# First head's block doubling planned later, the combination of the dilated groups spread out, a third work tile for the merge logits

## Chip, core and metric

One Trainium2 chip, one of its cores. The metric is the device time of one execution of the whole layer in microseconds (us), as the median of several runs. The input is x of 1 x 1024 x 1024 float32, the output has the same shape.

## What is computed

```python
x = x + 1/2 * SwiGLU_1(RMSNorm(x))
h = RMSNorm(x); cols = h @ w_in
A = dilated causal window attention   # 3 groups: window 128, 512, 2048 at dilation 1, 4, 16; 4 heads of 64 each
    # the three groups are weighted by their log-denominators:
    # y = sum_g softmax_g(lse_g) * o_g, per head
B = gated DeltaNet, 8 heads of 128, chunks of 64
    # per chunk: M = strict_lower(kbeta k^T * decay); u, w = (I + M)^-1 [vbeta, kbeta exp(g)]
    # scan: v_new = u - w S;  o = q_dec S + a_qk v_new;  S = exp(g_last) S + k_dec^T v_new
y = (sigmoid(g_a) * (A @ w_branch_a) + sigmoid(g_b) * (B @ w_branch_b)) @ w_out
x = x + y;  x = x + 1/2 * SwiGLU_2(RMSNorm(x));  final RMSNorm
```

All products are float32. The kernel splits an operand into a rounded high part and a low rest (H, L in the names) and adds three products HH, LH, HL, each a TensorE matmul of 128 x 128 on 512 columns.

## The kernel before, in words

The stages follow one another: FFN 1 (to about 735 us of the span), the mixer (to about 1790), `merge_out` (to about 2000), FFN 2.

**The mixer** has one loop of bulk work and a set of small tasks. Bulk work is `proj` (L229): a projection of h by 128 columns of w_in, 24 matmuls for each half of the tokens. Tasks are Python generators: attention blocks, `combine`, and for each DeltaNet head keys, decay, solve, scan and output. A planner (`Weave`) holds a planned time that each TensorE instruction advances by a cost written beside it. After every 9 or 12 bulk matmuls it runs the tasks that are due; a task issues its instructions up to its next `yield`, and the yielded number is how many planned us later it is due again. TensorE (PE) runs in exactly the order that comes out. The other engines' rows are ordered by priority (attention and `combine` first, then head 0, head 1, ..., bulk last). Each engine, and the DMA queue of SyncE (SP), executes its rows in order, so a row that waits holds up all rows behind it.

**One head** (h) goes: keys are projected, convolved (L927, DVE) and squared; `gdn_decay` makes Dm (cumulative sums on PE L1001, Exp on ACT L1003); `products` makes N (PE L1017, DVE L1019). `gdn_inverse_blocks` inverts the 32 x 32 diagonal blocks of all chunks: it stores N's blocks (L1075), loads them transposed into a tile M (SP, L1078), runs 68 small DVE rows, each on the result of the one before (L1087, L1088, L1100, L1101), stores the inverse (SP, L1109), loads it back as U (SP, L1114), and transposes U on DVE into Tm (L1116). M and Tm are made from the same tag "Tm", which has one buffer: M of head h + 1 can be loaded only when head h has read its Tm for the last time. `gdn_solve` then yields 57, scales two tiles (L1053), yields 5, and `gdn_merge` doubles the blocks to 64 and 128: PE L1136, DVE L1138, PE L1143, DVE L1145 and L1146, PE L1153 (the last reader of Tm), DVE L1155, PE L1161. Then w (PE L1061, ACT L1062) and the scan of 8 chunks (PE L1228, L1232, L1238, L1245; DVE L1230, L1243, L1249). PE's small products go to a few PSUM banks by tag: "tA" (L934, L1001, L1017, L1061, L838), "tM" for the doubling, "tC" for the scan; a bank is free again when DVE or ACT has read it. Results of L1017 are read by L1019.

**combine** weights the three groups of the attention, 8 tiles of 128 tokens. A tile loads oc (L815, two buffers of tag "xs"), runs 14 DVE rows (L820 to L834) and one Exp, yields 12, transposes on PE (L838), copies on ACT (L841) and stores (L842). It starts only once head 1 has its U, and pauses while a head is being made ready (`C.segs`, decay or values outstanding).

**merge_out** runs two halves of the tokens (a = 0, 1). For each of 8 columns f it loads the gate logits of both branches into a tile sgl (L1430, L1431; two buffers, tag "xs") and branch A's product (L1433), takes the sigmoid (ACT L1434), multiplies by B @ w_branch_b on PE, and adds on DVE (L1437 to L1439); the sum is split into mH (ACT L236) and mL (DVE L237), the last reader of sgl. Then 4 x 2 groups of 24 matmuls by w_out (PE L1456) read mH and mL, whose eighth column block f = 7 they need last. Weights come through `load_w2` (L203 load, L204 high part on ACT, L205 low part on DVE).

Of the kernel before, what the change touches and what calls it, by code (L numbers as in the profile page):

```python
# [9 lines left out]
F32 = mybir.dt.float32  # L10
# [6 lines left out]
P = 128  # L17
# [72 lines left out]
def psum(C, tag):  # L90
    return C.pp.tile([P, 512], F32, name=tag, tag=tag, bufs=BANKS[tag])
# [711 lines left out]
def combine(C):  # L803

    nc = C.nc
    while not C.attended or len(C.heads) < 2 or C.heads[1].U is None:
        yield 1.0
    for t in range(NT):

        while C.segs or any(X.D is None and X.ready for X in C.heads) or sum(not X.vals[1] for X in C.heads) > 1:  # L810
            yield 1.0
        C.combining = True
        oc = C.tp.tile([P, 792], F32, name="oc", tag="xs", bufs=2).rearrange("p (g q f) -> p g q f", g=3, q=2)
        for g in range(3):
            nc.sync.dma_start(oc[:, g], C.od[g][t * P:t * P + P])  # L815
        m, l = oc[:, :, :, 128:130], oc[:, :, :, 130:132]
        M = C.mx.tile([P, 1, 2, 2], F32, name="cM", tag="cM", bufs=2)
        e = C.mx.tile([P, 3, 2, 2], F32, name="ce", tag="ce", bufs=2)
        z = C.mx.tile([P, 3, 2, 2], F32, name="cz", tag="cz", bufs=2)
        nc.vector.tensor_tensor(out=M, in0=m[:, 0:1], in1=m[:, 1:2], op=ALU.max)  # L820
        nc.vector.tensor_tensor(out=M, in0=M, in1=m[:, 2:3], op=ALU.max)
        nc.vector.tensor_tensor(out=e, in0=m, in1=M.to_broadcast([P, 3, 2, 2]), op=ALU.subtract)
        nc.scalar.activation(e, e, AF.Exp, scale=0.125)
        nc.vector.tensor_tensor(out=z, in0=e, in1=l, op=ALU.mult)
        nc.vector.tensor_tensor(out=M, in0=z[:, 0:1], in1=z[:, 1:2], op=ALU.add)
        nc.vector.tensor_tensor(out=M, in0=M, in1=z[:, 2:3], op=ALU.add)
        nc.vector.reciprocal(M, M)
        nc.vector.tensor_tensor(out=e, in0=e, in1=M.to_broadcast([P, 3, 2, 2]), op=ALU.mult)
        for q in range(2):
            ov = oc[:, :, q, 0:128].rearrange("p g (h d) -> p g h d", d=64)  # L830
            nc.vector.tensor_tensor(out=ov, in0=ov, in1=e[:, :, q, :].unsqueeze(3).to_broadcast([P, 3, 2, 64]), op=ALU.mult)
        y = oc[:, 0, :, 0:128]
        for g in (1, 2):
            nc.vector.tensor_tensor(out=y, in0=y, in1=oc[:, g, :, 0:128], op=ALU.add)  # L834
        yield 12.0
        ps = psum(C, "tA")
        for f in range(2):
            C.weave.pe(nc.tensor.transpose(ps[:, f * P:f * P + P], y[:, f, :], C.ident), 0.11)  # L838
        C.combining = False
        yT = C.mx.tile([P, 2, P], F32, name="yT", tag="sc", bufs=6)  # L840
        nc.scalar.copy(yT, ps[:, :256].rearrange("p (f t) -> p f t", t=P))  # L841
        nc.sync.dma_start(C.yad[:, :, t * P:t * P + P], yT)  # L842


def gate_tile(C, w_in, c0, dst):
# [163 lines left out]
def products(C, X, src, sign):  # L1009

    nc = C.nc
    dst = t4c(C, "ka")
    for q in range(2):
        ps = psum(C, "tA")
        for i in range(4):
            c = q * 4 + i
            C.weave.pe(nc.tensor.matmul(ps[:, i * P:i * P + P], X.k[:, c, :], src[:, c, :], start=True, stop=True), 0.22)  # L1017
        cs = slice(q * 4, q * 4 + 4)
        nc.vector.scalar_tensor_tensor(dst[:, cs, :], ps.rearrange("p (c t) -> p c t", t=P), sign, X.D[:, cs, :],  # L1019
                                       op0=ALU.mult, op1=ALU.mult)  # L1020
    return dst


def gdn_solve(C, X):

    nc = C.nc
    h = X.h
    while X.D is None:
        yield 0.6
    rs, sv = rsqrt_cols(C, X.ssq[:, 0:8], 1.0, EPS, 8, "rg", w=24)  # L1030
    s, nk, ks = [X.cl[:, i] for i in range(3)]
    nc.vector.tensor_tensor(out=s, in0=rs, in1=rs, op=ALU.mult)
    nc.vector.tensor_tensor(out=s, in0=s, in1=C.beta[:, :, h], op=ALU.mult)
    for q in range(2):
        d = X.D[:, q * 4:q * 4 + 4, :]
        nc.vector.tensor_tensor(out=d, in0=d, in1=s[:, q * 4:q * 4 + 4].unsqueeze(2).to_broadcast([P, 4, P]), op=ALU.mult)
    nc.vector.tensor_tensor(out=nk, in0=rs, in1=sv, op=ALU.mult)
    nc.vector.tensor_tensor(out=ks, in0=s, in1=C.eS[:, :, h], op=ALU.mult)
    X.nk = nk
    yield 6.0  # L1040
    while X.prev and X.prev.prev and not X.prev.prev.scanned:
        yield 0.6
    X.N = products(C, X, X.k, -1.0)
    Tm, Um = gdn_inverse_blocks(C, X)
    yield INVERSE - 5.0
    while X.A is None:
        yield 0.6

    kg = t4c(C, "ka")
    for dst, sc in ((kg, C.eG[:, :, h]), (X.kd, ks)):  # L1050
        for q in range(2):
            cs = slice(q * 4, q * 4 + 4)
            nc.vector.tensor_tensor(out=dst[:, cs], in0=X.kd[:, cs], in1=sc[:, cs].unsqueeze(2).to_broadcast([P, 4, P]), op=ALU.mult)  # L1053
    yield 5.0
    yield from gdn_merge(C, X, Tm, Um)

    X.w = t4c(C, "ka")
    for q in range(2):
        ps = psum(C, "tA")
        for i in range(4):  # L1060
            C.weave.pe(nc.tensor.matmul(ps[:, i * P:i * P + P], kg[:, q * 4 + i, :], X.U[:, q * 4 + i, :], start=True, stop=True), 0.22)  # L1061
        nc.scalar.copy(X.w[:, q * 4:q * 4 + 4, :], ps.rearrange("p (c t) -> p c t", t=P))  # L1062
    yield STRETCH
    yield from gdn_scan(C, X)
# [99 lines left out]
    yield STRETCH  # L1164


INVERSE = 62.0


def gdn_values(C, w_in, X):  # L1170
# [225 lines left out]
def merge_out(C, tc, I, x2):  # L1396
# [25 lines left out]
    with tc.tile_pool(name="mp", bufs=1) as mp:  # L1422
        C.wp.add(mp, 0, 2)
        mH = mp.tile([P, 8, 512], F32R, name="mH")
        mL = mp.tile([P, 8, 512], F32R, name="mL")
        for a in (0, 1):
            ts = slice(a * 512, a * 512 + 512)
            for f in range(8):
                sg = C.tp.tile([P, 2, 512], F32, name="sgl", tag="xs", bufs=2)
                nc.sync.dma_start(sg[:, 0], C.sgad[f][:, ts])  # L1430
                nc.sync.dma_start(sg[:, 1], C.sgbd[f][:, ts])  # L1431
                pa = x2[a * 4 + f // 2][:, f % 2 * 512:f % 2 * 512 + 512]
                nc.sync.dma_start(pa, C.pad[f][:, ts])  # L1433
                nc.scalar.activation(sg, sg, AF.Sigmoid)  # L1434
                H, L = load_w2(C, cols(I["w_branch_b"], f * P), KT, P)
                pb = proj(C, H, L, a, "tC" if f % 2 else "mm")
                nc.vector.tensor_tensor(out=sg[:, 0], in0=sg[:, 0], in1=pa, op=ALU.mult)  # L1437
                nc.vector.tensor_tensor(out=sg[:, 1], in0=sg[:, 1], in1=pb, op=ALU.mult)
                nc.vector.tensor_tensor(out=sg[:, 0], in0=sg[:, 0], in1=sg[:, 1], op=ALU.add)  # L1439
                split_to(C, mH[:, f, :], mL[:, f, :], sg[:, 0])  # L1440
                if f % 2:
                    t = a * 4 + f // 2
                    nc.sync.dma_start(x2[t], C.x1d[t * P:t * P + P, :])
                if late and f:
                    late.pop(0)()
            for nh in (0, 1):
                W = []
                for k2 in range(0, 8, 2):
                    H, L = load_w2(C, I["w_out"][k2 * P:k2 * P + 256, nh * 512:nh * 512 + 512].rearrange("(k p) n -> p k n", p=P), 2, 512)
                    W += [(H[:, 0], L[:, 0]), (H[:, 1], L[:, 1])]  # L1450
                for t in range(4):
                    ps = psum(C, "tC" if t % 2 else "mm")
                    m = slice(t * P, t * P + P)
                    seq = [(mx, k, w) for k in range(8) for mx, w in ((mH, 0), (mH, 1), (mL, 0))]
                    for i, (mx, k, w) in enumerate(seq):
                        nc.tensor.matmul(ps, mx[:, k, m], W[k][w], start=i == 0, stop=i == len(seq) - 1)  # L1456
                    xs = x2[a * 4 + t][:, nh * 512:nh * 512 + 512]
                    nc.vector.tensor_tensor(out=xs, in0=xs, in1=ps, op=ALU.add)
                    if nh == 1:
                        late.append(normed(a * 4 + t))  # L1460
                        if a == 0 and len(late) > 2:
                            late.pop(0)()
                        if a == t == 1:
                            W = W + [first(n) for n in range(2)]
        C.wp.drop()
# [175 lines left out]
```

## Time and profile before

| | |
|---|---|
| runs of the kernel before | 2681.74, 2678.49, 2673.79 us; median 2678.49 |
| the profiled execution | 2679.78 us, its span 2678.0 us |
| mean granted TensorE clock | 0.987 of full |
| PE busy | 2585.1 us (97%) |
| DVE, ACT, POOL busy | 1461.4 (55%), 1025.5 (38%), 467.3 (17%) |
| DMA | 262.12 MB, mean 98 GB/s |

Times of the trace count from the span's start. The line behind an instruction is the kernel's line. An idle time stands in brackets with what ended it. The granted clock is a share of TensorE's full 2.4 GHz: 0.50 is 1.2 GHz.

### The profile page before, as it was taken

The numbers are of one execution on the slowest core, as the hardware profiler recorded it, in microseconds if no ns is written. First come the engines' busy times: TensorE is split into PE (matmuls) and PEld (weight loads), VectorE is DVE, ScalarE is ACT, GpSimd is POOL, SyncE is SP. The second block draws the span as 40 slices with busy tenths as digits, with TensorE's granted clock in tenths as the row PEclk, the third lists the DMA queues.
The fourth block names the chain that finished last, engine by engine and source line by source line (L and its number), as shares of the span: only waits on it lengthen the run. The fifth ranks groups of instructions, "written<-read, shape, count | busy, mean of one in ns | idle before, by whom it ended". The sixth has DMA issues, their size and how long they took to land. (4 is left out here: it accounts for less than half of the span.)

```text
span 2678.0 us, 34685 instructions
## 1 busy us (share of the span) xinstructions
PE 2585.1 (97%) x13007; PEld 2143.1 (80%) x13007; DVE 1461.4 (55%) x3276; ACT 1025.5 (38%) x1732; POOL 467.3 (17%) x378
## 2 busy tenths in 40 slices
PE   6999999999999999989899999999999999999997
PEld 5888888788788788777788888887877888887886
DVE  6444444432743457758768867435764444444326
ACT  5333333211544337435445434344433333333112
POOL 5534442000200000000000000000004445430002
PEclk9999999999999999999899999999999999999999
DMA  5323223531332231223222222357533222226311
GB/s 151 91 87 90 80 77 99 196 101 56 112 100 55 69 78 51 62 61 91 69 56 62 65 56 75 119 183 250 195 116 98 79 87 87 79 83 220 102 60 71
DMA packets 298810, 262.12 MB, mean 98 GB/s; under 512 B 39857, under 2 KB 232593, under 8 KB 298641
## 3 DMA queue, kind: packets, MB, share of 16 engines
q1 hardware_dynamic: 298640, 259.90, 31.9%
q8 instruction: 102, 1.67, 0.3%
q14 instruction: 68, 0.55, 0.1%
HBM read 195.26 MB, written 58.29 MB: 95 GB/s over the span
## 5 line engine op out<-in xcount | busy, mean ns | idle before, releaser
L229 PE MATMUL mm<-hH,wL 128*128 128x512 f32 x1072 | 444.1, 414 | 0.1
L229 PE MATMUL mm<-hL,wH 128*128 128x512 f32 x1072 | 422.7, 394 | 0.0
L229 PE MATMUL mm<-hH,wH 128*128 128x512 f32 x1072 | 421.3, 393 | 0.0
L204 ACT CAST wH<-wraw 128x1024 fp32r<-128x1024 f32 (+1 forms) x138 | 143.7, 1045 | 316.8 <-PE mm L537 124.3
L229 PEld LDWEIGHTS mm<-hL,wH 128*128 128x128 f32 x1072 | 202.9, 189 | 45.9
L229 PEld LDWEIGHTS mm<-hH,wL 128*128 128x128 f32 x1072 | 203.5, 190 | 44.4 <-issue 5.3
L229 PEld LDWEIGHTS mm<-hH,wH 128*128 128x128 f32 x1072 | 204.0, 190 | 35.7
L205 DVE TENSOR_TENSOR wL<-wraw,wH 128x1024 fp32r<-128x1024 f32 (+1 forms) x138 | 169.6, 1231 | 100.3 <-ACT wH L204 97.1
L355 DVE TENSOR_TENSOR wL<-wS,wH 128x1024 fp32r<-128x1024 f32 x88 | 126.9, 1443 | 161.3 <-ACT wH L354 160.5
L346 POOL TENSOR_TENSOR wS<-wraw 128x512 f32<-128x512 f32 x66 | 84.3, 1299 | 623.8 <-PE tA L296 383.0
L423 POOL TENSOR_TENSOR su<-su,sg 128x512 f32<-128x512 f32 x84 | 133.2, 1597 | 185.3 <-DVE su L397 161.2
L354 ACT CAST wH<-wS 128x1024 fp32r<-128x1024 f32 x88 | 92.5, 1053 | 152.2 <-PE tC L365 110.3
L393 ACT COPY ev<-mm 128x512 f32<-128x512 f32 (+1 forms) x118 | 68.5, 581 | 199.6 <-PE mm L365 199.6
L537 PE MATMUL mm<-wH,hidH 128*128 128x512 f32 x352 | 138.2, 393 | 3.1 <-DVE x L539 2.1
L537 PE MATMUL mm<-wH,hidL 128*128 128x512 f32 x352 | 137.9, 392 | 2.6 <-DVE hidL L205 2.6
L537 PE MATMUL mm<-wL,hidH 128*128 128x512 f32 x352 | 137.6, 391 | 1.3 <-DVE wL L205 1.3
L537 PE MATMUL tC<-wH,hidH 128*128 128x512 f32 x352 | 136.9, 389 | 1.7 <-ACT wH L204 1.7
L537 PE MATMUL tC<-wL,hidH 128*128 128x512 f32 x352 | 137.0, 389 | 0.5 <-DVE wL L205 0.5
L537 PE MATMUL tC<-wH,hidL 128*128 128x512 f32 x352 | 137.0, 389 | 0.0
L914 POOL MEMSET xp<- 128x3 f32 x24 | 2.4, 101 | 596.0 <-PE tA L775 249.6
L539 DVE SCALAR_TENSOR_TENSOR x<-mm,x 128x512 f32<-128x512 f32 x64 | 44.0, 688 | 104.0 <-PE mm L537 103.1
L539 DVE SCALAR_TENSOR_TENSOR x<-tC,x 128x512 f32<-128x512 f32 x64 | 44.0, 688 | 86.9 <-PE tC L537 86.9
(432 smaller groups left out, 6019.3 us busy)
## 6 DMA issues: line engine op xcount, KB each, us to landing
wraw<-in_w_in_dram SPq DMA_DIRECT2D x64, 512.0 KB, 4.0
wraw<-in_ffn_w_gate_dram SPq DMA_DIRECT2D x48, 512.0 KB, 4.6
hd<-su SPq DMA_DIRECT2D x84, 256.0 KB, 3.2
wraw<-in_ffn_w_down_dram SPq DMA_DIRECT2D x33, 512.0 KB, 4.4
wraw<-hd SPq DMA_DIRECT2D x33, 512.0 KB, 4.7
wraw<-in_ffn_w_up_dram SPq DMA_DIRECT2D x26, 512.0 KB, 4.9
xs<-in_ffn_w_up_dram SPq DMA_DIRECT2D x22, 512.0 KB, 3.9
wraw<-in_w_branch_b_dram SPq DMA_DIRECT2D x16, 512.0 KB, 4.6
```

The source lines that it names most:

```text
L204: nc.scalar.copy(H[:, :width], raw[:, :width])
L205: (nc.gpsimd if C.pool_split else nc.vector).tensor_tensor(out=L[:, :width], in0=raw[:, :width], in1=H[:, :width].bitcast(F32), op=ALU.sub ...
L229: ins = nc.tensor.matmul(ps, w[:, k, :], x[:, k, :], start=k == 0 and i == 0, stop=k == kt - 1 and i == 2)
L346: nc.gpsimd.tensor_tensor(out=out, in0=p, in1=q, op=op)
L354: nc.scalar.copy(H[:, :n], srcs)
L355: eng.tensor_tensor(out=L[:, :n], in0=srcs, in1=H[:, :n].bitcast(F32), op=ALU.subtract)
L393: nc.scalar.copy(v[:, s], ps[:, s])
L423: (eng or C.nc.gpsimd).tensor_tensor(out=out, in0=out, in1=sg, op=ALU.mult)
L537: nc.tensor.matmul(ps, h[:, m], w, start=i == 0, stop=i == len(seq) - 1)
L539: nc.vector.scalar_tensor_tensor(xs, ps, 0.5, xs, op0=ALU.mult, op1=ALU.add)
L914: nc.gpsimd.memset(xp[:, 0:3], 0.0)
```

## The change

Three edits. In `combine` the pause before the transposes goes from 12 to 14 planned us, and another pause of 14 stands after each tile's store, so that two tiles are at least 28 planned us apart. The first head (the one without `X.prev`) waits 9 planned us more before its L1053 rows and its doubling. In `merge_out` every third tile sgl is taken from the stage's own pool with one buffer, beside the two of tag "xs". No matmul or DVE row is added or taken away; ACT has two rows fewer, loads of its function table. Lines behind the second edit count one more than before, behind the last two more.

```diff
--- before.py
+++ after.py
@@ -832,7 +832,7 @@
         y = oc[:, 0, :, 0:128]
         for g in (1, 2):
             nc.vector.tensor_tensor(out=y, in0=y, in1=oc[:, g, :, 0:128], op=ALU.add)
-        yield 12.0
+        yield 14.0
         ps = psum(C, "tA")
         for f in range(2):
             C.weave.pe(nc.tensor.transpose(ps[:, f * P:f * P + P], y[:, f, :], C.ident), 0.11)
@@ -840,6 +840,7 @@
         yT = C.mx.tile([P, 2, P], F32, name="yT", tag="sc", bufs=6)
         nc.scalar.copy(yT, ps[:, :256].rearrange("p (f t) -> p f t", t=P))
         nc.sync.dma_start(C.yad[:, :, t * P:t * P + P], yT)
+        yield 14.0
 
 
 def gate_tile(C, w_in, c0, dst):
@@ -1042,7 +1043,7 @@
         yield 0.6
     X.N = products(C, X, X.k, -1.0)
     Tm, Um = gdn_inverse_blocks(C, X)
-    yield INVERSE - 5.0
+    yield INVERSE - 5.0 + (0.0 if X.prev else FIRST)
     while X.A is None:
         yield 0.6
 
@@ -1164,7 +1165,7 @@
     yield STRETCH
 
 
-INVERSE = 62.0
+INVERSE, FIRST = 62.0, 9.0
 
 
 def gdn_values(C, w_in, X):
@@ -1426,7 +1427,8 @@
         for a in (0, 1):
             ts = slice(a * 512, a * 512 + 512)
             for f in range(8):
-                sg = C.tp.tile([P, 2, 512], F32, name="sgl", tag="xs", bufs=2)
+                where, tag, n = (mp, "sgl", 1) if (a * 8 + f) % 3 == 2 else (C.tp, "xs", 2)
+                sg = where.tile([P, 2, 512], F32, name="sgl", tag=tag, bufs=n)
                 nc.sync.dma_start(sg[:, 0], C.sgad[f][:, ts])
                 nc.sync.dma_start(sg[:, 1], C.sgbd[f][:, ts])
                 pa = x2[a * 4 + f // 2][:, f % 2 * 512:f % 2 * 512 + 512]
```

**On PE**, head 0's doubling starts 36 bulk matmuls later (row 4817 of PE's order, row 4781 before), and head 1's almost where it was (row 4964, 4967 before). Between head 0's last L1153 and head 1's first L1136 there were 117 bulk matmuls and 22 small ones of the scan; now there are 90 and 14. The transposes of two successive tiles of `combine` had 27 to 90 bulk matmuls between them and now have 90 to 189; tiles 5 to 8, which stood between the doublings of heads 2 and 3, now stand between those of heads 3 and 5.

**SP, head 1's inverse from the blocks' store to their load.** In the kernel before (gt is a gate's logits, g is head 0's output, ud1 and U are head 1's):

```order
L1109 DMA ud1_111<-fsT_8841 256x1x32 [waits DMAHW0_49,DVE_49,Pool_49]
L1109 DMA ud1_111<-fsT_8841 256x1x32 [waits DMAHW1_49]
L1109 DMA ud1_111<-fsT_8841 256x1x32 [waits DMAHW2_49]
L1109 DMA ud1_111<-fsT_8841 256x1x32 [waits DMAHW3_49]
L854 DMA sgad1_85<-gt_9442 128x512 [waits Activation_49]
L1279 DMA ybd0_100<-g_8792 128x512 [waits DMAHW5_49,DVE_49]
L1114 DMA U_8916<-ud1_111 32x8x32 [waits DMAHW3_49,DMAHW2_49,DMAHW6_49,DMAHW1_49,DMAHW0_49]
L1114 DMA U_8916<-ud1_111 32x8x32 [waits DMAHW7_49]
L1114 DMA U_8916<-ud1_111 32x8x32 x2
```

and in the change:

```order
L1110 DMA ud1_111<-fsT_8841 256x1x32 [waits DMAHW2_49,DVE_49,Pool_49]
L1110 DMA ud1_111<-fsT_8841 256x1x32 [waits DMAHW3_49]
L1110 DMA ud1_111<-fsT_8841 256x1x32 [waits DMAHW4_49]
L1110 DMA ud1_111<-fsT_8841 256x1x32 [waits DMAHW5_49]
L1115 DMA U_8916<-ud1_111 32x8x32 [waits DMAHW5_49,DMAHW4_49,DMAHW6_49,DMAHW3_49,DMAHW2_49]
L1115 DMA U_8916<-ud1_111 32x8x32 [waits DMAHW7_49]
L1115 DMA U_8916<-ud1_111 32x8x32 [waits DMAHW0_49]
L1115 DMA U_8916<-ud1_111 32x8x32 [waits DMAHW1_49]
L1280 DMA ybd0_100<-g_8792 128x512 [waits DVE_49]
```

The load of U now follows its store at once; the stores of a gate and of head 0's output (L1279, L1280 with the shift) have moved from in front of it to behind. Ahead of this place the load of M (Tm_8836) waits for a DVE and a PE semaphore in both kernels.

**PE, head 2's doubling and head 3's keys** (ka_10559 and ka_10600 are the convolved keys or queries of head 3, tA_10751 to tA_10757 the banks of head 3's N). In the kernel before:

```order
L1136 MATMUL tM_10730<-Tm_10082,ka_9979 32x32 [waits DVE_49]
L1136 MATMUL tM_10730<-Tm_10082,ka_9979 32x32 x15
L1017 MATMUL tA_10751<-ka_10463 128x128 [waits PE_49]
L1017 MATMUL tA_10751<-ka_10463 128x128 x3
L1017 MATMUL tA_10757<-ka_10463 128x128 [waits PE_49,Activation_49]
L1017 MATMUL tA_10757<-ka_10463 128x128 x3
L934 MATMUL tA_10855<-ident_61,ka_10559 128x128 [waits DVE_49,Activation_49]
L934 MATMUL tA_10855<-ident_61,ka_10559 128x128 x3
```

and in the change, where the four L1018 rows stand 6 bulk matmuls ahead of this piece:

```order
L229 MATMUL mm_10722<-hH0_3514,wL_10717 128x512
L229 MATMUL mm_10722<-hH0_3514,wH_10716 128x512
L229 MATMUL mm_10722<-hL0_3515,wH_10716 128x512
L1154 MATMUL tM_10906<-Tm_10124,ka_10021 64x64 [waits DVE_49]
L1154 MATMUL tM_10906<-Tm_10124,ka_10021 64x64 x3
L1154 MATMUL tM_10913<-Tm_10124,ka_10021 64x64 [waits DVE_49,PE_49]
L1154 MATMUL tM_10913<-Tm_10124,ka_10021 64x64 x3
L935 MATMUL tA_10920<-ident_61,ka_10600 128x128 [waits DVE_49,PE_49,Activation_49]
L935 MATMUL tA_10920<-ident_61,ka_10600 128x128 x3
```

L934, which takes the bank that L1019 must have read, stood right behind the products of N; it now stands behind L1153 (L1154 with the shift).

**SP, the end of the first half's gate logits in merge_out** (sgad7 and sgbd7 are those of f = 7, sgad0 those of the next half, w_out's tiles come in the order of use). In the kernel before:

```order
L203 DMA wraw_16062<-in_w_out_dram 128x2x512 [waits DMAHW6_49,DMAHW0_49,DVE_49]
L1430 DMA sgl_15937<-sgad5_89 128x512 [waits DMAHW7_49,DVE_49]
L1431 DMA sgl_15937<-sgbd5_97 128x512
L203 DMA wraw_16068<-in_w_out_dram 128x2x512 [waits DMAHW2_49,DMAHW1_49]
L1433 DMA x24_15716<-pad0_75 128x512
L1433 DMA x24_15716<-pad1_76 128x512 [waits DMAHW3_49]
L203 DMA wraw_16074<-in_w_out_dram 128x2x512 [waits DMAHW6_49,DMAHW4_49,DVE_49]
L1443 DMA x22_15719<-x1d_71 128x1024 [waits DMAHW5_49,DVE_49]
L1430 DMA sgl_15979<-sgad6_90 128x512 [waits Activation_49]
L1431 DMA sgl_15979<-sgbd6_98 128x512 [waits DMAHW7_49]
L203 DMA wraw_16080<-in_w_out_dram 128x2x512 [waits DMAHW1_49,DMAHW0_49,DVE_49]
L1430 DMA sgl_16020<-sgad7_91 128x512 [waits DVE_49]
```

and in the change:

```order
L203 DMA wraw_16062<-in_w_out_dram 128x2x512 [waits DMAHW3_49]
L1432 DMA sgl_16020<-sgad7_91 128x512 [waits DMAHW4_49,DVE_49]
L1433 DMA sgl_16020<-sgbd7_99 128x512 [waits DMAHW5_49]
L203 DMA wraw_16068<-in_w_out_dram 128x2x512 [waits DMAHW7_49,DMAHW6_49]
L1435 DMA x24_15716<-pad0_75 128x512
L1435 DMA x24_15716<-pad1_76 128x512 [waits DMAHW0_49]
L203 DMA wraw_16074<-in_w_out_dram 128x2x512 [waits DMAHW3_49,DMAHW1_49,DVE_49]
L1445 DMA x23_15721<-x1d_71 128x1024 [waits DMAHW2_49,DVE_49]
L203 DMA wraw_16080<-in_w_out_dram 128x2x512 [waits DMAHW6_49,DVE_49]
L1432 DMA sgl_16438<-sgad0_84 128x512 [waits DMAHW4_49]
L1433 DMA sgl_16438<-sgbd0_92 128x512 [waits DMAHW5_49]
L203 DMA wraw_16190<-in_w_out_dram 128x2x512 [waits DMAHW1_49,DVE_49]
```

The load for f = 7 stood behind the fourth tile of w_out; it now stands behind the first.

## Rows read from the trace of the kernel before

**Rows 1.** The page's part 1: busy time and share of the span.

```profile
PE 2585.1 (97%) x13007; PEld 2143.1 (80%) x13007; DVE 1461.4 (55%) x3276; ACT 1025.5 (38%) x1732; POOL 467.3 (17%) x378
```

**Rows 2.** Waits of PE, 1085 to 1400 us: total, times, longest.

```profile
PE tA L934 <- DVE ka L1019: 11.9, 2, 9.8
PE tM L1136 <- DVE Tm L1116: 6.0, 1, 6.0
PE tA L838 <- issue: 3.0, 1, 3.0
PE tA L1061 <- ACT ka L1062: 1.3, 1, 1.3
PE tA L1061 <- ACT Dm L1003: 1.2, 1, 1.2
```

**Rows 3.** Windows: length, PE busy, granted clock, DMA share, GB/s.

```profile
1160.00:1164.00 4.00, 3.74 (x41) 0.50 0.01 4
1164.00:1168.00 4.00, 4.00 (x18) 0.62 0.00 0
...
1298.00:1302.00 4.00, 4.00 (x10) 0.50 0.59 150
1302.00:1304.00 2.00, 2.00 (x19) 0.61 0.00 0
```

**Rows 4.** Timeline of PE around heads 0 and 1: start, length, instruction [idle].

```profile
1110.67 0.40 PE L229 MATMUL mm<-hH,wL 128*128 128x512 f32 x1
...
1111.82 0.39 PE L229 MATMUL mm<-hL,wH 128*128 128x512 f32 x1
1112.13 1.14 PE L1153 MATMUL tM<-Tm,ka 64*64 64x64 f32 x16
...
1160.26 0.98 PE L1136 MATMUL tM<-Tm,ka 32*32 32x32 f32 x16 [6.01 <-DVE Tm L1116]
```

**Rows 5.** Timeline of SP's queue, head 1's inverse.

```profile
1113.31 1.71 SPq L1078 DMA_DIRECT2D Tm<-nbd  x4
...
1150.27 2.53 SPq L1109 DMA_DIRECT2D ud<-fsT  x4
...
1154.97 0.34 SPq L1279 DMA_DIRECT2D ybd<-g  x1
1155.50 1.85 SPq L1114 DMA_DIRECT2D U<-ud  x4
```

**Rows 6.** Timeline of DVE, head 1's inverse, and head 2's L1116 to head 3's L1019.

```profile
1117.58 0.28 DVE L1087 TENSOR_TENSOR fsP<-fsT,Tm 128x120 f32<-128x120 f32 x1 [1.50 <-DMA Tm<-nbd]
...
1150.05 0.16 DVE L1088 TENSOR_TENSOR fsT<-fsT,fsP 128x4 f32<-128x4 f32 x1
...
1270.87 1.24 DVE L1116 STREAM_TRANSPOSE Tm<-U 128x1024 f32<-128x1024 f32 x1
...
1284.79 0.86 DVE L1138 COPY W<-tM 32x256 f32<-32x256 f32 x2
...
1290.84 0.17 DVE L186 TENSOR_TENSOR rgt<-rgy 128x8 f32<-128x8 f32 x1
...
1293.92 1.29 DVE L1019 SCALAR_TENSOR_TENSOR ka<-tA,Dm 128x512 f32<-128x512 f32 x2
```

**Rows 7.** The merge: timelines of DVE and SP, PE's waits, windows as in 3.

```profile
1837.17 0.68 DVE L237 TENSOR_TENSOR mL<-sgl,mH 128x512 fp32r<-128x512 f32 x1
...
1837.88 0.32 SPq L1430 DMA_DIRECT2D sgl<-sgad  x1
...
PE mm L1456 <- ACT mH L236: 3.4, 1, 3.4
PE mm L1456 <- DVE mL L237: 0.6, 1, 0.6
...
1842.00:1846.00 4.00, 3.38 (x15) 1.00 0.92 316
...
1850.00:1852.00 2.00, 1.88 (x5) 0.50 0.97 301
```

## Prediction

> **What bounds the kernel now.** I read the page's busy times first. The reader is to see that PE is busy for nearly the whole span and no other engine is near that [rows 1]. So the order of PE can hardly be made shorter, and what a change of order can win or lose is the idle time of PE and the slow clock behind it. Next I read the waits of PE in the mixer between the first head's solve and the fourth's, because there the change moves rows [rows 2]. Four stalls stand out: 9.8 us for head 3's N (PE needs a bank that L1019 has not read), 6.0 us for head 1's Tm, 3.0 us before a transpose of `combine`, and 2.5 us in two parts before w (L1061). Then the windows behind two of them [rows 3]. After the 6.0 us PE runs at 0.50 from 1160 to 1164 and at a mean of 0.62 to 1168, which gives away 4 x 0.50 + 4 x 0.38 = 3.5 us of full clock. After the 9.8 us PE resumes at about 1294.8, is at 0.50 until 1302 and at 0.61 until 1304, which gives away 7.2 x 0.50 + 2 x 0.39 = 4.4 us. A stall of PE costs its length and 3 to 4 us more. Last come the timelines that say why a stall ends where it does [rows 4 to 6], and the merge [rows 7].
>
> All sums are made against the profiled execution, 2679.8 us, which lies 1.3 us above the median of the three runs. A measurement can tell about 0.3% from no change, here 8 us.
>
> **Term A: head 1's Tm, +7.5 us.** Head 0's doubling moves behind 36 more bulk matmuls. Five of them take 1111.82 - 1110.67 = 1.15 us [rows 4], so one 0.23 and 36 of them 8.3 us. Head 1's own doubling stays where it was in PE's order. The two are tied by a buffer: head 1's M is loaded into the buffer from which head 0's L1153 reads. The trace shows it: L1153 runs from 1112.13 to 1113.27 [rows 4], and the load of M is issued at 1113.31 [rows 5]. The DVE chain starts when it has landed, at 1117.58, and its last row starts at 1150.05 [rows 6]. Then the store (1150.27), the load of U (1155.50, [rows 5]), the transpose, and PE starts at 1160.26 after 6.01 us idle [rows 4]. From the load of M to PE that is 46.95 us. In the change the load comes at 1113.3 + 8.3 = 1121.6. One thing shortens the chain: on SP the load of U no longer stands behind the store of head 0's output, issued at 1154.97. The four stores of the inverse are issued by 1152.80, so the load of U could start between 0 and 2.5 us earlier than 1155.50; I take 1. So PE starts at 1121.6 + 46.0 = 1167.6. It arrives at 1160.26 - 6.01 = 1154.25, perhaps half a us earlier with three rows fewer ahead. The idle time becomes about 13.5 us, 7.3 more. The clock is at half after the 6 us already, so a longer stall adds only the difference of the two cases above, at most 0.9; I take 0.2. Bounds: +9 if nothing is shortened, and 0 if DVE is through with the chain 8 us sooner. That isn't excluded: the chain is 68 rows of 0.28 us at the start and 0.16 at the end, some 15 us in all, within 32.6, so more than half of the stretch is other DVE work, part of which could have been done before the chain starts. I take the upper part, since DVE's order around the chain is otherwise nearly unchanged.
>
> **Term B: the 3.0 us before a transpose, 0.** In both orders two tiles of `combine` stand on DVE ahead of head 2's L1019, whose bank the transpose takes. PE's distance and DVE's work shrink alike. Bounds: -4.5 us (gone with its clock) and +2.
>
> **Term C: head 3's N, -6.5 us.** Before, L934 stands right behind the products of N, which follow L1136 at once, and DVE comes to L1019 at 1293.92 to 1295.21 [rows 6]. That costs 9.8 us and 4.4 of clock, 14.2. In the change L934 stands behind L1153, and 27 bulk matmuls (6.2 us) stand between L1136 and it where there were none. But the spacing leaves two tiles of `combine` between L1116 and L1019, and the doubling's DVE rows now stand there too: the two copies that read L1153's result (by the two of L1138, 0.86 us), then the rows from L186 on, 1290.84 to 1295.21 or 4.4 us [rows 6]. PE has just done L1153 when it meets L934, so it idles at least 5.2 us. By the 3.5 us of clock behind 6.0, I put 2.8 behind that: 8.0 in place of 14.2. I take -6.5, a little over the difference, since a 0.6 us wait nearby goes too. Bounds: -14.2 if other work fills the gap, +5 under the second rival.
>
> **Term D: w of head 3, -2 us.** L1061, directly behind L1001, waited for L1001's Exp on ACT (Dm L1003) and then for the copy that ACT does behind it (L1062) [rows 2]. In the change L1001 stands ahead of L1161, and 9 bulk matmuls (2.1 us) stand between. The 2.5 us idle mostly goes. L1189 now follows L1001 and can inherit a part, so 0 is the other end and -4 (with the clock) the near one.
>
> **Term E: the later tiles, +1 us.** Tiles 5 to 8 now stand beside heads 3 to 5, where they can get ahead of an L1019. Bounded by 0 and by the 3.0 us that two tiles cost before [rows 2].
>
> **Term F: the third tile, -4 us.** The load of f = 7 is issued at 1837.88, right after f = 5's mL at 1837.17 has freed its tile. PE then waits 3.4 us for mH and 0.6 for mL of f = 7, and from 1850 to 1852 it has half the clock, 1.0 us [rows 7]. With the third tile the load waits for f = 4 instead, one f earlier, and three loads of w_out move behind it. Full gain 5.0. The DMA engines are 0.92 busy there [rows 7], so moving one load ahead pushes others back; I take 4. Bounds: -5.0 and 0.
>
> The ACT table loads saved and the 14 for 12 cost nothing that PE sees. The mixer's end stays covered: branch A's last projections fill PE there, and if that cover were gone the last head's 2 us would show.
>
> Sum: 7.5 - 6.5 - 2 + 1 - 4 = -4 us. Profiled 2675.8; by the median 2678.5 - 4 = **2674.5 us**. Its own range, by half of the terms' doubts, is 2668 to 2681.
>
> **The rivals.**
>
> *Head 1's stall doesn't grow.* DVE does the scan and convolution rows that stood in the chain before the chain begins, and the chain takes 39 us in place of 47. For it: more than half of the stretch is other work. Against it: those rows depend on projections that PE makes only then. A is 0: 2667 us, and 2659 if head 3's N comes in time as well.
>
> *Slower: head 3's N comes later, not sooner.* Mechanism: between L1116 (1270.87) and the end of L1019 (1295.21) DVE needs 24.3 us [rows 6]; now the doubling's rows stand in that piece as well, four rows and the wait for PE in each round, 5 us or so. If DVE reaches L1116 no earlier against PE than before, PE idles some 15 us in place of 9.8. The tipping point is whether DVE has done the second tile's rows before the projection that the convolution behind them needs. For it: two tiles still stand there and `combine` has priority over every head. Against: those projections now end 10 planned us later, which gives DVE the time. Then C is +5, D 0, E 2, F -4, A 7.5: 10.5 slower, 2689 us.
>
> *The third tile does nothing.* The merge is bound by its transfers: 316 GB/s at 0.92 busy [rows 7]. If every us of PE's wait is a byte that has to come anyway, the wait moves from mH to a w_out tile and F is 0: 2678.5 us. The Trainium skill, "DMA: Bandwidth & Descriptors", section Specifications, puts the limit of one core's share of HBM at about 358 GB/s and of its 16 DMA engines at 435, which speaks against this edit. Here the window shows 316 with the engines nearly always busy, so the trace is close to that rule without deciding it. That less urgent loads for w_out's second half stand behind f = 7 decides for me against it.
>
> **How the numbers follow.** The forecast has 0.40, the first rival 0.27, the slower one 0.18, the third 0.15. The forecast's range lies mostly within 2670.5 to 2686.5: 0.13 of it is faster, 0.27 the same. The first rival is faster. The second is slower. Of the third 0.13 is the same, 0.02 slower by E. That makes faster 0.40, same 0.40, slower 0.20. The range takes in most of the first rival and the low part of the second: 2660 to 2688.
>
> **What would show it.** Right: PE's wait for Tm before head 1's L1136 near 13 us, with the load of M issued near 1122; the wait for L1019 before head 3's L934 near 5; no wait of 3 us for mH of f = 7. Wrong in A: the wait for Tm at 7 or less. Wrong in C: a wait for ka of L1019 above 10, or none. Wrong in F: PE waiting for a w_out tile (L204 or L205) at the start of L1456. The whole would be wrong if stalls of over 3 us appear beside heads 4 to 7, where the trace of before shows none that I priced.

## The result, and the profile after

The changed kernel takes 2686.94 us (15 runs, 2682.92 to 2691.76), the kernel before 2680.82 (15 runs beside it). The ratio is 1.0024 with a 95% interval of 1.0016 to 1.0033, so 4 to 9 us slower, where 4 us faster were forecast. The profiled execution took 2683.5 us (a span of 2681.8), 3.4 below the median. In it the stages ahead of the stretch below happened to be 2.4 us shorter than in the profile before, so times in the mixer are to be compared after adding 2.4.

PE's waits in the mixer, changed kernel, 1085 to 1400 us, the answer to [rows 2]: total, times, longest.

```profile
PE tM L1137 <- DVE Tm L1117: 14.0, 1, 14.0
PE tA L935 <- DVE ka L1020: 10.4, 3, 4.4
PE tA L1190 <- ACT vb L1191: 1.3, 1, 1.3
PE tA L1190 <- ACT U L1163: 0.6, 1, 0.6
```

The same view from 1400 to 1780 us, where the kernel before has no wait above 0.7:

```profile
PE tA L935 <- DVE ka L1020: 3.4, 1, 3.4
PE tA L1190 <- ACT vb L1191: 1.3, 1, 1.3
PE tA L1190 <- ACT U L1163: 0.9, 2, 0.5
PE tA L935 <- ACT ka L929: 0.8, 1, 0.8
```

Head 1's wait for Tm has gone from 6.0 to 14.0. Before and after, the waits of L934 (L935 with the shift) for L1019 (L1020) hold one of 2.1, just ahead of the stretch that is used below. Head 3's wait of 9.8 has become one of 4.4. The 3.0 before a transpose, which was a wait for L1019 too, is now 3.9 before an L935. One of 3.4 has come beside head 4's doubling. The two waits before w have become waits of L1190.

The chain behind the 14.0 us, changed kernel, timelines of PE and SP, as in [rows 4, 5]:

```profile
1116.31 1.14 PE L1154 MATMUL tM<-Tm,ka 64*64 64x64 f32 x16
...
1162.21 1.01 PE L1137 MATMUL tM<-Tm,ka 32*32 32x32 f32 x17 [13.99 <-DVE Tm L1117]
```

```profile
1117.48 1.73 SPq L1079 DMA_DIRECT2D Tm<-nbd  x4
...
1157.58 1.82 SPq L1115 DMA_DIRECT2D U<-ud  x4
```

The load of M again starts as head 0's last L1154 ends (1117.45). From it to PE's start are 44.7 us, 46.95 before. PE arrived at 1162.21 - 13.99 = 1148.2.

PE's waits in the merge, changed kernel, 1840 to 1865 us, for [rows 7]:

```profile
PE mm L1458 <- ACT mH L236: 1.7, 1, 1.7
PE mm L1458 <- DVE mL L237: 0.3, 1, 0.3
```

So 2.0 us in place of 4.0 in this profile.

To sum up a kernel in the mixer I take the stretch between two waits that every kernel has: the first L934 behind head 0's L1019 (1091.12 us before) and the first L877 that waits (1775.77). It holds the same work in all of them (3991 or 3992 matmul records). One view of windows gives its length and PE's busy time; the difference is PE's idle time, and since the work is the same, a difference in busy time is a difference in clock. Kernel before, kernel changed (length, PE busy, mean granted clock, DMA):

```profile
1091.12:1775.77 684.65, 658.27 (x3992) 0.98 0.27 75
```

```profile
1088.76:1779.92 691.16, 657.53 (x3991) 0.97 0.26 75
```

The change adds 6.5 us here: idle time goes from 26.4 to 33.6, busy time is alike.

### The profile page after: what moved, and what is told of

It reads as the page before. It is cut to its first block, busy times and chain, and to the rows that moved or that the text cites. A ratio compares the mean times of both kernels' runs of the same rounds, so it can differ in the third digit from the quotient of the medians.

```text
span 2681.8 us, 34675 instructions
## 1 busy us (share of the span) xinstructions
PE 2580.8 (96%) x13007; PEld 2138.7 (80%) x13007; DVE 1463.2 (55%) x3276; ACT 1022.1 (38%) x1730; POOL 466.1 (17%) x378
```

## The experiments

Each kernel was timed in five rounds beside the kernel before (2679 to 2680 us in these). The table holds the median, the ratio to the kernel before with its interval, and the mixer's stretch with PE's idle and busy us from one profile each.

| kernel | median | ratio [95%] | stretch | idle | busy |
|---|---|---|---|---|---|
| before | 2679 to 2681 | 1 | 684.7 | 26.4 | 658.3 |
| changed | 2686.9 | 1.0024 [1.0016, 1.0033] | 691.2 | 33.6 | 657.5 |
| e_first | 2685.0 | 1.0023 [1.0013, 1.0032] | 688.0 | 31.8 | 656.3 |
| e_spread | 2684.7 | 1.0024 [1.0015, 1.0034] | 685.5 | 26.0 | 659.5 |
| e_third | 2680.4 | 1.0002 [0.9994, 1.0011] | 679.4 | 25.7 | 653.7 |
| e_nofirst | 2682.9 | 1.0013 [1.0005, 1.0022] | 685.9 | 26.1 | 659.8 |
| e_early | 2686.5 | 1.0024 [1.0016, 1.0033] | 685.7 | 24.9 | 660.8 |
| e_earlythird | 2669.9 | 0.9966 [0.9953, 0.9979] | 673.0 | 18.1 | 654.9 |
| e_earlyonly | 2668.8 | 0.9959 [0.9946, 0.9972] | 671.2 | 19.1 | 652.2 |
| e_second | 2668.6 | 0.9961 [0.9948, 0.9974] | 670.5 | 16.2 | 654.3 |
| e_notile_before | 2666.6 | 0.9952 [0.9938, 0.9967] | 665.3 | 16.4 | 649.0 |
| e_notile_spread | 2677.8 | 0.9998 [0.9989, 1.0007] | 678.0 | 22.0 | 656.0 |
| e_secondsp | 2675.1 | 0.9987 [0.9976, 0.9997] | 677.9 | 20.7 | 657.2 |
| e_mix | 2676.4 | 0.9989 [0.9979, 0.9999] | 679.5 | 23.0 | 656.5 |

A caution on single profiles: e_third has the mixer of the kernel before, row for row, and nearly its idle time, but 4.6 us less busy time. So the clock of one execution is chance to some us. The idle time repeats better: e_spread and e_nofirst, which have one order of the mixer, show 26.0 and 26.1. What follows rests on medians, on idle time, and on stalls by name.

**The three edits one by one.** e_first takes the edit of the doubling alone, e_spread the two pauses of `combine` alone, e_third the third tile alone; e_nofirst is the changed kernel with this undone:

```diff
-    yield INVERSE - 5.0 + (0.0 if X.prev else FIRST)
+    yield INVERSE - 5.0
```

> The kernel before with the first head's 9 planned us alone. Theory (the buffer ties head 1's inverse to head 0's doubling): PE's wait for Tm of head 1 is 13 to 14 us in place of 6.0, and the time is 7 to 9 us over the kernel before; head 3's wait for L1019 stays between 5 and 10. Rival (the spacing of the tiles is what costs, and the longer wait lets DVE catch up and is paid back behind it): at most 3 us slower.

Measured: 5.9 us slower. PE waits 14.0 us for Tm in e_first as in the changed kernel, to 0.01 us. Head 3's wait for L1019 falls to 2.4, so "between 5 and 10" missed, but one of 4.2 for ka L928 comes ahead of it; and 4.1 stand before head 2's L934 in place of the 3.0. The tie by the buffer holds. The time is below the 7 to 9 of the theory, though the interval (3.5 to 8.6) reaches into it; the rival's "at most 3" is just outside. Its ratio, 1.0023, is also that of the changed kernel, 1.0024: the other two edits together add nothing here that the intervals can tell.

> The kernel before with the spaced tiles of combine alone. Theory: PE's wait for head 1's Tm stays near 6, head 3's wait for L1019 falls from 9.8 to 4 or 5, waits of some 3 us for L1019 and 1 to 2 us before L1189 (L1190 with the shift) appear in heads 3 to 5; in all 0 to 4 us faster. Rival (the spacing is what costs): 4 us slower or more, with waits for L1019 in heads 3 to 5 that sum to more than what head 3 gains.

Measured: 5.5 us slower, so here my theory falls. The waits of e_spread in the stretch, 1090 to 1780 us:

```profile
PE tA L935 <- ACT ka L929: 6.6, 2, 4.5
PE tM L1137 <- DVE Tm L1117: 5.8, 1, 5.8
PE tA L1190 <- ACT vb L1191: 4.0, 2, 2.8
PE tA L1190 <- issue: 3.2, 1, 3.2
PE tA L935 <- DVE ka L1020: 2.2, 2, 2.1
PE tA L1190 <- ACT U L1163: 2.1, 3, 1.5
```

The 9.8 of head 3 and the 3.0 at the transpose are gone, as wanted: only 4.5 is left of them. But the idle sum is what it was (26.0 against 26.4), since waits before L1190, L935 and L1002 in heads 3 to 6 have come in their place. And there are more of them: nine places of 1 us or more inside the stretch in place of six, five of 2 us or more in place of three.

> The kernel before with the third tile sgl alone. Theory: PE's waits for mH and mL of f = 7 fall from 4.0 to about 2 us as in the changed kernel, 2 us faster or a little more with the clock. Rival (the merge is bound by its transfers): no difference within 1 us, the wait turning up elsewhere in the merge.

Measured: no difference (1.3 us slower, interval from 1.6 faster to 2.9 slower). PE's waits in its merge, 1830 to 1860 us, and a window of it:

```profile
PE mm L1457 <- ACT mH L236: 1.2, 1, 1.2
PE mm L1457 <- DVE wL L205: 1.2, 2, 0.7
PE mm L1457 <- ACT wH L204: 0.9, 1, 0.9
```

```profile
1840.00:1844.00 4.00, 2.42 (x10) 1.00 0.96 348
```

The wait for mH and mL fell from 4.0 to 1.2, and waits for w_out's tiles of 2.1 us came: 3.3 in all. The two other pairs show the same: mH 5.5 in e_spread, 1.7 and 2.5 for w_out's tiles in e_nofirst; mH 4.5 in e_earlyonly, 1.7 and 2.6 in e_earlythird. The medians of the three pairs differ by +1.3, -1.8 and +1.1 us. The rival is right in the main: in this window the DMA engines are busy 0.96 of the time and move 348 GB/s, and what comes earlier for f = 7 comes later for w_out.

> The changed kernel without the first head's 9 planned us (spaced tiles and third tile). Theory: the two add up, 2 to 6 us faster than the kernel before, and head 1's wait for Tm is near 6 us. Rival (the spacing is what costs): within 2 us of the changed kernel, some 4 us slower than the kernel before.

Measured: 3.8 us slower than the kernel before, 4.0 faster than the changed one (2.3, when each is set against the kernel before beside it). The rival is nearer. The edits don't add up: alone they cost 5.9, 5.5 and about 1 (which is within the noise), together 6.

**Head 0's doubling the other way, and head 1's.** If the buffer of Tm ties head 1's inverse to head 0's doubling, an earlier head 0 must free PE, and a later head 1 as well.

```diff
-INVERSE, FIRST = 62.0, 9.0
+INVERSE, FIRST = 62.0, -12.0
```

e_earlyonly is the kernel before with the first head's edit at this value, e_earlythird has the third tile too, e_early also the spaced tiles. e_second is the kernel before with 8 planned us more for head 1 alone:

```diff
-    yield INVERSE - 5.0
+    yield INVERSE - 5.0 + FIRST.get(X.h, 0.0)
...
-INVERSE = 62.0
+INVERSE, FIRST = 62.0, {0: 0.0, 1: 8.0}
```

e_secondsp has these lines in the changed kernel, and e_mix is e_second with -6 for head 0 and 4 for head 1.

> The kernel before with the first head's doubling 12 planned us earlier, nothing else. Theory: PE's wait of 6.0 for head 1's Tm goes, with some 3 us of half clock behind it, 6 to 10 us faster than the kernel before. Rival (the idle time is only moved): within 3 us, with a larger wait for L1019 of head 2 or 3.

Measured: 11 us faster than the kernel before (interval 7.5 to 14.5). No wait of PE for Tm is left in it, and the idle sum is down by 7.3. That is a little over the 6 to 10 of the theory, which the interval covers.

> The kernel before with head 1's doubling 8 planned us later, head 0's as it was. Theory (head 1's stall is a fixed chain of 47 us that PE has too little other work for): the wait of 6.0 for Tm goes because PE does bulk work in it; 3 to 9 us faster. Rival (DVE is what is short, and PE only meets it later): the wait for L1019 of head 2 or 3 grows by as much, within 3 us of the kernel before.

Measured: 11 us faster as well (7 to 14), over the 3 to 9 of the theory. Head 1's chain isn't shortened: from the load of M to the transpose it takes 47.75 us, 45.65 before [rows 5] with the transpose at 1158.96. SP's and DVE's timelines of e_second:

```profile
1111.77 1.71 SPq L1078 DMA_DIRECT2D Tm<-nbd  x4
```

```profile
1159.52 1.24 DVE L1116 STREAM_TRANSPOSE Tm<-U 128x1024 f32<-128x1024 f32 x1
```

PE comes to L1136 at 1161.7, after it, and does bulk work until then. Head 3's 9.8 shrinks too, to 4.6 and 1.5. Of the 10.2 us less idle time 6.0 are the wait for Tm and 3.7 are head 3's. So the stall was a chain of nearly fixed length with too little bulk work beside it, and either end can be moved.

> The kernel before with the first head 12 earlier and the third tile, without the spacing. Theory (the spacing only moves stalls to heads 3 to 5): 2 us or more faster than the same kernel with the spacing, 7 to 11 faster than the kernel before. Rival (the spacing pays once head 1's stall is out of the way): slower than with it.

> The changed kernel with the first head's doubling 12 planned us earlier than before (FIRST = -12 in place of +9). Theory (the buffer of Tm ties head 1 to head 0): PE's wait for head 1's Tm is 0 to 1 us in place of 14.0, and the kernel is 10 us or more faster than the changed one, 4 to 10 faster than the kernel before. Rival (PE's idle time in the mixer is only moved: DVE is behind and the next wait takes it over): the idle sum of the mixer stays within 3 us of that without the 9, and so does the time.

Measured: e_earlythird is 10 us faster than the kernel before, e_early 7 us slower: beside the early first head the spacing costs 16.7 us. In e_early the wait for Tm is gone, as the theory said, but nothing is gained by it. Its idle sum is within 3 us of e_nofirst's, as the rival said (24.9 and 26.1), and its time is 3.6 us over it. With the spaced tiles and the third tile the time is 2683 to 2687 us whether head 0 is early by 12, in place, or late by 9.

> The changed kernel with head 1 later by 8 in place of head 0 by 9 (spaced tiles and third tile kept). Theory (the spacing breaks what head 1's moved doubling gives): 8 us or more slower than the same without spacing and third tile (2668.6), so 2677 or more. Rival (what cost 17 us beside the early first head was a chance of that order): within 5 us of 2668.6.

Measured: 6.5 us slower than e_second, with the spacing and the third tile. A little under the 8 of the theory, a little over the 5 of the rival: the spacing costs here too (the third tile by itself cost nothing that could be told), but the amount depends on the order that it meets.

> The kernel before with head 0's doubling 6 planned us earlier and head 1's 4 later. Theory (what counts is the room between the two doublings): head 1's wait for Tm is 0 to 1 us and the time is that of the two kernels that gave the room from one side, 2665 to 2671. Rival (each of these orders has its own stalls, the room is only part): more than 4 us away from them.

Head 0 earlier by 6 and head 1 later by 4 leaves no wait for Tm, but is only 3 us faster than the kernel before. The rival is right: the room between the two doublings is needed, and what the heads behind make of it is another matter. Its trace has waits of 5.0 for L1019 and of 1.0 to 2.2 us in seven places.

**What it is in the spacing: tile rows, or PE's order.** e_notile_before and e_notile_spread are the kernel before and e_spread without the tiles' own rows on DVE (12 of each tile; the text above says 14) and ACT. PE's order stays that of the full kernel in each. A tile's loads, transposes, copy and store stay too.

```diff
-        m, l = oc[:, :, :, 128:130], oc[:, :, :, 130:132]
...
-            nc.vector.tensor_tensor(out=ov, in0=ov, in1=e[:, :, q, :].unsqueeze(3).to_broadcast([P, 3, 2, 64]), op=ALU.mult)
         y = oc[:, 0, :, 0:128]
-        for g in (1, 2):
-            nc.vector.tensor_tensor(out=y, in0=y, in1=oc[:, g, :, 0:128], op=ALU.add)
```

> The kernel before without the tiles' own work: the DVE rows L820 to L834 and the Exp L823 of combine are left out (so the groups are not weighted and only the first one's values go on); loads, transposes, stores, planned times and PE's order are as before. Both theories: faster than the kernel before, by the stalls in which tile rows stand ahead of L1019: head 3's 9.8 us falls to 3 or less and the 3.0 at the transpose goes; 6 to 14 us.

> The same left out from the kernel with the spaced tiles alone, whose PE order also stays. Theory (the spacing costs through PE's order: the heads 3 to 6 come out in another phase, and the stalls there need no tile rows): still 3 us or more slower than its partner without the spacing, with the stalls before L1190 near 1539 and 1633 us still there. Rival (the spacing costs through the tiles' rows on DVE and ACT, which now stand ahead of heads 3 to 5): within 2 us of its partner, and those stalls are gone.

Measured: without the tiles' rows the kernel before is 13 us faster, with the spacing 7 us faster (2684.7 to 2677.8). So the spacing does what it is for: the tiles' rows cost PE 6 us less. But with those rows in neither kernel, the spaced order is 11.2 us slower than the other. That is the order of the rows: PE's, and with it DVE's, which the two traces show to differ as well. It outweighs the gain by 5 us, which is what e_spread lost. The stretch in the two (without, then with the spacing):

```profile
1093.81:1759.14 665.33, 648.98 (x3991) 0.99 0.27 77
```

```profile
1093.89:1771.93 678.04, 656.00 (x3992) 0.98 0.26 76
```

5.7 of the 12.7 us are idle time and 7.0 are slower matmuls. How much of the 7.0 belongs to the order is open, since the profile with the spacing took 3.9 us more than its kernel's median, the one without it just the median. Where 3.2 of the idle time come from shows at one place, beside head 6's doubling. Kernel before, timeline of PE without the bulk rows:

```profile
1629.15 1.14 PE L1161 MATMUL tM<-U,W 64*64 64x64 f32 x16
1630.28 2.05 PE L1189 MATMUL tA<-vb,U 128*128 128x128 f32 x16
...
1633.01 2.05 PE L1017 MATMUL tA<-ka 128*128 128x128 f32 x16 [0.18 <-ACT vb L1190]
```

The same in e_notile_spread, whose lines count 17 less (L1144 for L1161, L1000 for L1017, L1172 for L1189), with DVE's L1002 for L1019:

```profile
1622.70 1.14 PE L1144 MATMUL tM<-U,W 64*64 64x64 f32 x16
1623.77 2.05 PE L1000 MATMUL tA<-ka 128*128 128x128 f32 x16
1629.04 3.52 PE L1172 MATMUL tA<-vb,U 128*128 128x128 f32 x16 [3.22 <-issue]
```

```profile
1628.25 1.29 DVE L1002 SCALAR_TENSOR_TENSOR ka<-tA,Dm 128x512 f32<-128x512 f32 x2
```

and the granted clock behind the wait:

```profile
1629.00:1632.00 3.00, 2.96 (x14) 0.50 0.23 38
```

The next head's products of N have come ahead of this head's L1189. They fill both banks of "tA", and DVE reads these only when it has made the scale for them, from 1628.25 on, 2.4 us after the products' end. In the kernel before L1189 comes first, L1019 begins at 1634.2, while the products still run, and nothing waits for it. The same 3.2 us stand in e_spread at the same place (1633.2), 150 us after DVE began its last tile (1479.6). No tile is near. The pauses of `combine` moved the doublings of heads 3, 5 and 6 behind 9 more bulk matmuls, about 2 planned us, and which task is polled first came out differently.

**The changed kernel beside e_first.** This order is not the changed kernel's. There the doublings of all heads stand at the same bulk matmul as in e_first; with the tiles' transposes set aside, PE's two orders differ in four rows alone, the L1001 of one head. So what the spacing does in the changed kernel is done by the tiles, their rows and transposes, and hardly by the order of the heads' products. Timelines of DVE and PE beside head 4's doubling, changed kernel:

```profile
1463.36 0.15 DVE L820 TENSOR_TENSOR cM<-oc 128x4 f32<-128x4 f32 x1
...
1469.54 1.02 DVE L831 TENSOR_TENSOR oc<-oc,ce 128x384 f32<-128x384 f32 x2
...
1471.95 0.42 DVE L834 TENSOR_TENSOR oc<-oc 128x256 f32<-128x256 f32 x1
...
1476.22 1.29 DVE L1020 SCALAR_TENSOR_TENSOR ka<-tA,Dm 128x512 f32<-128x512 f32 x2
```

```profile
1472.41 1.20 PE L1154 MATMUL tM<-Tm,ka 64*64 64x64 f32 x16
1477.06 1.08 PE L935 MATMUL tA<-ident,ka 128*128 128x128 f32 x4 [3.45 <-DVE ka L1020]
```

The same place in e_first, where no tile stands and L1019 begins at 1477.95:

```profile
1477.93 1.14 PE L1153 MATMUL tM<-Tm,ka 64*64 64x64 f32 x16
1479.00 0.66 PE L934 MATMUL tA<-ident,ka 128*128 128x128 f32 x4
```

The tile's 12 rows take 3.6 us of DVE, and PE waits 3.4 us where it waited nothing. Against e_first the spacing wins 2.1 us of idle time at head 3's N and loses 4.2 behind 1400 us. The changed kernel without the tiles' rows was not run.

## Why the prediction was wrong

By idle time in the two profiles the terms came to A +8.0, B +0.9, C -5.4, D -0.5, E +4.8 and F -2.0, in all +5.8, beside 6.1 us between the medians and -4 forecast. PE's busy time in the stretch is alike, so the clock adds nothing to this sum.

**Term A** was right: 13.5 us idle forecast, 13.99 measured, by the tie that the text named. The load of M started 0.03 to 0.04 us after the end of L1153 (L1154), in both kernels. Three errors inside cancelled, which was luck: counted from the same point, the load of M came 1.8 us sooner than I said, the chain was shorter by 2.2 where I took 1 (the rows allowed up to 2.7, not 2.5), and PE arrived over 3 us sooner.

**Term B** was forecast at 0. The wait at the transpose went, and one of 3.9 us for the same L1019 stands before head 2's L934 (1228 us): 0.9 more, within the bounds.

**Term C** was right to 1 us: 5.2 idle forecast, 4.4 measured in place of 9.8, for the reason given. DVE's L1156 copies run at 1303.4 and L1020 ends at 1308.7, 5.3 us after. The order that does it comes with the first head's edit, since e_first has it too; with the tiles' rows still ahead of L1019 there it leaves 6.6.

**Term D** was half right: L1190 inherits 1.9 of 2.4 us, as the text allowed.

**Term E is the step that failed most**: "the later tiles, +1 us", "bounded by 0 and by the 3.0 us that two tiles cost before". In the changed kernel the idle time from 1400 to 1780 us grew from 3.3 to 8.2 us, 4.8 in place of 1 and over the bound. 3.4 of them are one wait for L1020 beside head 4, behind a tile's rows. That is the mechanism that the term named; the size was wrong, since the bound was taken from one place where two tiles stood, and a single tile at another place cost more. It is also the sign that the text gave for the whole being wrong, a stall of over 3 us beside heads 4 to 7. A second cost of the spacing the term had at nothing: that a pause in one task can swap the small products of other tasks hundreds of us later. Where the first head isn't moved, that alone costs 11 us (the two kernels without tile rows). I compared the orders around heads 0 to 3 and took the rest as unchanged.

**Term F failed too**: -4 forecast. The stall fell by 2.0 us in the changed kernel's profile, and alone the edit gives nothing (-1.6 to 2.9 us). The third rival, bound transfers, with 0.15, was what happened, and its sign, a wait that moves from mH to a w_out tile, was the right one to look for. The figure beside it was not the reason. The Trainium skill gives about 358 GB/s as the limit of one core's share of HBM ("DMA: Bandwidth & Descriptors", Specifications). These runs go beyond it, and the measurement decides: e_third moves 420 GB/s in a window of FFN 2.

```profile
2432.00:2436.00 4.00, 4.00 (x13) 0.69 1.04 420
```

What the merge shows is the busy share, 0.92 and 0.96 at 316 and 348 GB/s while PE waits. I had read the 0.92, and put the order of the loads above it.

The slower rival named another mechanism (head 3's N later), and that did not happen. So the forecast's main terms A and C held to about a us. Of the 10 us between the forecast and the result E holds 3.8, F 2.0 (4 by the run of the third tile alone), D 1.5, C 1.1, B 0.9 and A 0.5.

The times that beat both kernels were found on the way: e_second and e_earlyonly, each one number at one place, at 2668.6 and 2668.8 us.

## What to carry to other kernels

When a table or a planner makes an engine's order, compare the whole order before and after, not the neighbourhood of the edit: look for small products whose banks are freed by a long chain (here N's) and that have come ahead of products which wait for nothing. Where work is moved, count its rows at the new place against the slack there, not at a price from the old place. A wait behind a chain of fixed length goes when one end of the chain is moved against the bulk work; lengthening the side that feeds it does the opposite. A buffer more didn't help a stretch whose transfer engines were already busy 0.92 to 0.96 of the time.

## What the runs showed that I had not expected

The same 3991 matmuls of the mixer took from 649 to 661 us of PE's busy time over these kernels, and 653.7 and 658.3 in two profiles of one and the same order. The idle sum of the stretch was the same in the kernel before and in e_spread, 26 us, and yet their medians lie 5.5 us apart. What makes this difference is open: the busy times of the two profiles differ by 1.2 us, PE's wait for mH in the merge by 1.5 or more (5.5 in e_spread), and one profile of each is too few. Which of the planner's polls swaps the products beside head 6 was not tried.
